# Hybrid attention block on one core: the high parts' cast moved directly behind the exponential, the gates' products behind the low parts

## The chip, the cores and the metric

One core of a Trainium2 chip runs the whole kernel. The metric is the device time of one execution in microseconds (us). The kernel before took 439.7 us as the median of 3 runs (439.3 to 441.55 us).

## The reference, cut to what matters

One encoder layer over 1024 tokens of width 1024. A single projection gives the columns of two head groups. Group A is two-dimensional neighbourhood attention (8 heads, a window of 8 x 16 on a grid of 16 rows and 64 columns, with a learned relative bias). Group B is windowed grouped-query attention (8 query heads, 2 key/value heads, |i - j| <= 128, rotary positions, a sink logit in the softmax). Each group's output is multiplied by SiLU of its gate columns, the two are concatenated and projected, and a LayerNorm follows.

```
h = einsum('bsd,de->bse', x, w_in)
q_a, k_a, v_a, z_a, q_b, k_b, v_b, z_b = split(h)
y_a = neighborhood_attention(q_a, k_a, v_a, rel_pos_bias)
y_b = windowed_gqa_with_sink(rotary(q_b), rotary(k_b), v_b, sink)
mixed = concatenate([y_a * silu(z_a), y_b * silu(z_b)])
x = layer_norm(alpha * x + einsum('bse,ed->bsd', mixed, w_out), ln_gain, ln_bias)
```

## The kernel before, in words

Float32 values are carried as a sum of two float16 parts, a high part (the rounded value) and a low part (the value less its high part), so that TensorE multiplies float16 tiles in three products. The program has three stretches: a first one of about 122 us that projects the values, scales the weights and projects the first six column blocks; the attention loop, from about 122 to 364 us; and the output projection with its LayerNorm. The change lies in the loop.

The loop at the end of `hybrid_block` (lines 1445 to 1536) runs over 128 blocks of scores, here numbered 0 to 127: group B first (blocks 0 to 63, four pairs of heads p of 16 blocks), then group A (64 to 127). In each step i the code issues, in this order:

- `stage_qk` for block i: TensorE forms the scores in a bank of `ps_s` (lines 889 and 890; there are four such banks), and VectorE masks them and takes the row's minimum `nm` (line 905, into `sn`);
- every fourth step `stage_ot` and `stage_pv`: m is the place in a group of four steps. At m = 0 TensorE transposes a finished group of outputs (line 1006, every second time) and multiplies the transposed probabilities `tr` of four blocks by the values (line 968), in banks of `ps_t`, of which there are two. `stage_pv` of group q comes at step 4q + 9, so the last of its four blocks has six steps to arrive. At m = 1 `stage_on` divides by the row sums (lines 977 and 984);
- `stage_z`: for group B the gates' product, four VectorE instructions per transposed bank (line 993). Two stand directly behind the transposes at m = 0; one at the head of each of the steps m = 2 and m = 3 (line 1454), ahead of that step's scores;
- up to two VectorE instructions from a queue, above all the low parts of the projected queries and keys (line 310, two per half of a column block, written `ks` or `qs`);
- `stage_tr` for block i - 1: ScalarE casts the probabilities to their high part (line 939, `split`), VectorE makes the low part from both (line 940), and a transposing DMA on SyncE's queue writes `tr` (line 942). `split` has six buffers, `tr` nine;
- ScalarE work with priority 0 from a queue, among it the first cast of a pair of queries or keys (line 304);
- `stage_exp` for block i: ScalarE's exponential, back into the block's bank of `ps_s` (line 921), in group B with the row sum read from the accumulator;
- more ScalarE work from the queue: the second cast of the pair of queries or keys (line 304; VectorE's line 310 waits for both), casts of weights (line 241, for which GpSimd then makes the low parts, lines 246 and 247), of rotated queries (line 306, GpSimd's line 312 behind them), of gated outputs (line 1171) and others;
- GpSimd's work, and between these the matmuls of the projections (line 443), dealt out evenly over the steps.

Each engine executes its own instructions in the order in which they are issued, so a step's order in the code is the order in each engine's queue. A block's way is thus: scores, `sn` with `nm`, exponential, high part, low part, transposing DMA, values.

Of the kernel before, what the change touches and what calls it, by code (L numbers as in the profile page):

```python
# [12 lines left out]
AF = mybir.ActivationFunctionType  # L13
ALU = mybir.AluOpType
# [10 lines left out]
PSCALE = 2.0 ** 14  # L25
# [40 lines left out]
def hybrid_block(ctx, tc, xT, x, wt, wv, wo, bias, sink, gain, lbias, cos, sin, bmask, out):  # L66
    nc = tc.nc
# [118 lines left out]
    def book(eng, work):  # L186
        if clock["step"] is not None:
            due[eng] = max(due[eng], at_step(clock["step"]))
        due[eng] += work
# [4 lines left out]
    def pop(eng, n, top=1, same=False):  # L194
        q = queues[eng]
        ready = [op for op in q if op.prio <= top and all(
            d.step is not None and d.step + d.lag < clock["step"] + (same and op.prio == 0 and d.eng == "act")
            and (eng != "sp" or d.fin + 1.0 < at_step(clock["step"]))
            and (eng != "act" or d.eng != "pool" or d.fin < at_step(clock["step"])) for d in op.deps)]
        for op in sorted(ready, key=lambda op: op.prio)[:n]:  # L200
            q.remove(op)
            op.emit()
# [622 lines left out]
    units = unit_list()  # L825
# [6 lines left out]
    st = {}  # L832
# [78 lines left out]
    def stage_exp(u):  # L911
        c = used(u)
        c = slice(c[0], c[1] + (u[0] == "b"))
        book("act", 0.2 + 0.0008 * (c.stop - c.start) + (0.2 if u[0] == "b" else 0))
        sn, nm = st.pop((u, "sn")), st.pop((u, "nm"))
        pt = st.pop((u, "ps"))
        k = units.index(u) % 4
        if k == 0 and u[0] == "b":
            st[units.index(u) // 4, "sm"] = ap.tile([128, 4], F32, tag="sm", name="sm", bufs=4)
        acc = st[units.index(u) // 4, "sm"][:, k:k + 1] if u[0] == "b" else None  # L920
        nc.scalar.activation(pt[:, c], sn[:, c], AF.Exp, bias=nm, scale=-1.0, accum_out=acc)  # L921
        st[u, "p"] = pt

    def stage_tr(u):
        n, m = geom(u)
        pt = st.pop((u, "p"))
        hl = split[units.index(u) % NSPLIT]
        c = slice(*used(u))
        book("act", 0.06 + 0.00086 * (c.stop - c.start))
        book("dve", 0.07 + 0.00108 * (c.stop - c.start))  # L930
        s = 384 - 128 * m
        if u[0] == "b":
            b = b_span(u)[0]
            if b == 7:
                nc.vector.memset(hl[:, 384:448], 0.0)
            if b == 4 and u[1] > 0:
                nc.vector.memset(hl[:, 320:384], 0.0)
        h, l = (hl[:, o + c.start:o + c.stop] for o in (s, 384))
        nc.scalar.activation(h, pt[:, c], AF.Copy, scale=PSCALE)  # L939
        nc.vector.scalar_tensor_tensor(l, pt[:, c], PSCALE, h, op0=ALU.mult, op1=ALU.subtract)  # L940
        tr = ap.tile([128, 6, 128], F16, tag="tr", name="tr", bufs=BH)
        nc.sync.dma_start(tr[:, :2 * m, :], hl[:, s:s + 256 * m], transpose=True)
        st[u, "tr"] = tr
# [42 lines left out]
    def stage_z(n):  # L986
        for _ in range(n if st.get("z") else 0):
            ps, k, h, e, m = st["z"].pop(0)
            o = ps.rearrange("p (b h c) -> p b h c", h=2, c=64)
            r = slice(64 * e, 64 * e + 64)  # L990
            z = zt[k][r, 512 * h:512 * h + 512].rearrange("p (b m c) -> p b m c", m=2, c=64)[:, :, m]
            book("dve", 0.42)
            nc.vector.scalar_tensor_tensor(z, o[64 * m:64 * m + 64, :, e], z_col(k)[r], z, op0=ALU.mult, op1=ALU.mult)

    def stage_ot(q):
        g, p, j, h = quad(q)
        if g == "b":
            j, h = h, j
        if j == 0:
            return  # L1000
        need(*stk_ops.get(f"zb{p}" if g == "b" else f"z{p}", ()))
        ps = bank("t")
        book("dve", 0.67 if g == "a" else 0)
        o = on.pop((g, p, h))
        for i in range(4):
            nc.tensor.transpose(ps[:, 128 * i:128 * i + 128], o[:, 2 * i:2 * i + 2].rearrange("p h e -> p (h e)"), identf)  # L1006
        if g == "b":
            st["z"] = [(ps, 4 + p, h, e, m) for e in range(2) for m in range(2)]
            stage_z(2)
        else:  # L1010
            z = zt[p].rearrange("p (r c) -> p r c", c=GW)[:, :, 32 * h:32 * h + 32]
            nc.vector.scalar_tensor_tensor(z, ps.rearrange("p (c r) -> p r c", r=ROWS), z_col(p), z,
                                           op0=ALU.mult, op1=ALU.mult)
# [204 lines left out]
    LT, LP = LTT, LPP  # L1218
# [226 lines left out]
    for i in range(-LD, NU + LO):  # L1445
        if 0 <= i + LD < NU:
            stage_load(units[i + LD], i)
        if i < 0:
            continue
        clock["step"] = i  # L1450
        per, h = divmod(i, 16)
        bulk["step"] = i
        if (i - LP - 3) % 4 > 1:
            stage_z(1)
        if i == VA_AT:
            gather_v(0)
        if i in SCAN_LD:
            n, b = divmod(NSCAN + SCAN_LD.index(i), 4)
            wo_load(SCAN[n], b, *scans[-4:-3])
            wo_scan(SCAN[n], b)  # L1460
        if i >= T_GO and i % 4 == 0 and len(scans) == 16 and all(op.step is not None and op.fin + 3 < at_step(i) for op in scans):
            wo_scale()
            scans.clear()
            t_prep(0)
            for b in range(4):
                wo_load(1, b, t_low[(0, 1, 3, 2)[b]])
            t_prep(1)
        if i in B_LD:
            n = B_LD.index(i)
            b_load(n, w_ops[NL - 5 + n] if n < 5 else b_ops[n - 5])  # L1470
        if i in B_AT:
            b_split(B_AT.index(i))
        if i in M_AT:
            m_queue(M_AT.index(i))
        if i == M2_AT:
            m_kq(2, ("A11", "A12", "A21", "A22"))
        if i == M3_AT:
            m_kq(3, ("A11", "A21"))
        if i == 129:
            t_soon(0)  # L1480
            x_soon(0)
            t_soon(3)
            x_soon(4)
            x_soon(1)
            t_soon(1)
            t_soon(2)
        if bulk["last"] == i:
            sp_at.append(i)
        if i >= 118:
            pop("sp", 3)  # L1490
        elif sum(j > i - 3 for j in sp_at) < 2:
            kept = len(queues["sp"])
            pop("sp", 1)
            if len(queues["sp"]) < kept:
                sp_at.append(i)
        if i < NU:
            u = units[i]
            if u[0] == "b" and u[3] == 0:
                need(*[o for j in range(2) for o in stk_ops[f"b{u[1]}", j, u[2]]])
            if u[0] == "a" and u[3] == 0:  # L1500
                need(*stk_ops[u[1], u[2], 0], *stk_ops[u[1], u[2], 1])
            stage_qk(u)
        q, m = divmod(i - LP - 3, 4)
        if i >= Q30 + 2:
            q, m = (NU // 4 - 2, i - Q30 - 2) if i < Q30 + 4 else divmod(i - LP - 3, 4)
        elif i >= Q30:
            q, m = -1, 0
        if m == 0 and 0 <= q - 1 < NU // 4:
            stage_ot(q - 1)
        if m == 0 and 0 <= q < NU // 4:  # L1510
            stage_pv(q)
        kept = len(queues["dve"])
        pop("dve", 2, 0)
        if m > 1 and len(queues["dve"]) == kept and i not in DVE_ADD and i < DVE_ADD[-1] and due["dve"] + DVE_OWN < at_step(i + 1):
            fill_in("dve")
        if 0 <= i - LT < NU:
            stage_tr(units[i - LT])
        pop("act", 1, 0)
        pump_to(i + F1)
        if 0 <= q < NU // 4:  # L1520
            g, p, j, h = quad(q)
            if g == "a" and p < 3 and (j, h, m) == VA_STEP:
                gather_v(p + 1)
        if m == 1 and 0 <= q < NU // 4:
            stage_on(q)
        pop("dve", ND, same=True)
        if i < NU:
            stage_exp(units[i])
        held = [op.prio for op in queues["act"] if op.prio <= 1]
        pop("act", NA if 0 in held or i < 105 and len(held) < 5 else 2)  # L1530
        pop("pool", NP)
        for eng in ("pool", "act", "dve")[:3 if i in DVE_ADD or len(scans) and i <= T_GO + 8 else 2]:
            for _ in range(2):
                if free_at(eng, ROOM[eng]):
                    fill_in(eng)
        pump_to(i + 1)
# [78 lines left out]
```

## Time and profile before

| | |
|---|---|
| median of 3 runs | 439.7 us (439.3 to 441.55) |
| the profiled execution, its whole time | 440.44 us |
| its span, first to last instruction | 438.6 us |
| VectorE instructions for the gates' product (line 993) | 32, 15.4 us in all |
| casts of queries and keys on ScalarE (line 304) | 32, 576 to 592 ns each |
| low parts of queries and keys on VectorE (line 310) | 32, 677 to 695 ns each |
| transposing DMA, issue to landing | 2.3 to 6.5 us, median 3.7 |

The profile is of one execution. An engine's busy time is the time in which it had an instruction under way; PE is TensorE's matmuls, PEld its weight loads, which run beside them, DVE is VectorE, ACT ScalarE, POOL GpSimd and SPq SyncE's DMA queue. In a row of the waits stand the time waited in all, the number of waits and the longest. In a row of the timeline stand the start in us, the duration in us, engine, line and tiles, how many instructions are merged into the row, and in brackets the engine's idle time ahead of it with what ended it.

### The profile page before, as it was taken

The numbers are of one execution on the slowest core, as the hardware profiler recorded it, in microseconds if no ns is written. First come the engines' busy times: TensorE is split into PE (matmuls) and PEld (weight loads), VectorE is DVE, ScalarE is ACT, GpSimd is POOL, SyncE is SP. The second block draws the span as 40 slices with busy tenths as digits, with TensorE's granted clock in tenths as the row PEclk, the third lists the DMA queues.
The fourth block names the chain that finished last, engine by engine and source line by source line (L and its number), as shares of the span: only waits on it lengthen the run. The fifth ranks groups of instructions, "written<-read, shape, count | busy, mean of one in ns | idle before, by whom it ended". The sixth has DMA issues, their size and how long they took to land.

```text
span 438.6 us, 9414 instructions
## 1 busy us (share of the span) xinstructions
PE 431.6 (98%) x3225; PEld 252.7 (58%) x3225; DVE 335.3 (76%) x852; ACT 309.9 (71%) x665; POOL 280.8 (64%) x300
## 2 busy tenths in 40 slices
PE   9999999999999999999999998999999999999996
PEld 8997754444445655565656564655656555444445
DVE  5977976775967888988888897978787755675455
ACT  5849789668678988787978769888889773332321
POOL 0100074668438658779988899797989881058585
PEclk9999999999999999999999999999999999999999
DMA  8922469995329999875899999989899969811113
GB/s 272 404 84 61 137 231 334 242 292 177 124 47 196 205 187 206 190 160 123 138 169 235 188 188 218 212 184 191 142 198 220 169 121 339 332 48 73 72 73 121
DMA packets 128817, 80.10 MB, mean 183 GB/s; under 512 B 97280, under 2 KB 106496, under 8 KB 128768
## 3 DMA queue, kind: packets, MB, share of 16 engines
q1 hardware_dynamic: 128624, 79.30, 75.3%
q8 instruction: 25, 0.41, 0.4%
q14 instruction: 24, 0.20, 0.1%
q10 hardware_dynamic: 144, 0.20, 0.1%
HBM read 47.97 MB, written 8.42 MB: 129 GB/s over the span
## 4 chain that ended last, share of the span: by engine, by line
PE 78%; POOL 5%; DMA 5%; ACT 4%; DVE 4%; issue 3%; SPq 0%; POOLq 0%; ACTq 0%
PE ps_pj L443 36%; PE ps_s L1240 8%; PE ps_s L550 6%; PE ps_t L968 6%; PE ps_pj L1240 4%; PE ps_s L889 3%; PE ps_s L890 3%; PE ps_pj L550 3%; PE ps_t L550 3%; PE ps_t L1240 2%; DMA vd<-vt 2%; DMA ws<-in_wt 2%; POOL xr L1349 2%; POOL xr L1350 2%; PE ps_t L1006 1%
## 5 line engine op out<-in xcount | busy, mean ns | idle before, releaser
L443 PE MATMUL ps_pj<-xf,wh 128*128 128x512 f16 x672 | 201.4, 379 | 0.0
L443 PE MATMUL ps_pj<-xf,wl 128*128 128x512 f16 x336 | 127.3, 379 | 0.0
L443 PEld LDWEIGHTS <-wh 128*128 128x128 f16 x672 | 63.6, 98 | 59.0 <-issue 1.1
L921 ACT ACTIVATE ps_s<-sn,nm 128x321 f32<-128x321 f32 (+3 forms) x128 | 68.4, 535 | 35.0 <-DVE nm L905 34.4
L940 DVE SCALAR_TENSOR_TENSOR split<-ps_s,split 128x320 f16<-128x320 f32 (+2 forms) x128 | 63.6, 497 | 19.5 <-ACT split L939 17.8
L246 POOL TENSOR_SCALAR wr<-wr,wsc 128x512 f32<-128x512 f32 x32 | 22.9, 715 | 67.8 <-ACT wh L241 63.7
L939 ACT ACTIVATE split<-ps_s 128x320 f16<-128x320 f32 (+2 forms) x128 | 55.5, 434 | 1.5
L443 PEld LDWEIGHTS <-wl 128*128 128x128 f16 x336 | 32.8, 98 | 37.9
L905 DVE CUSTOM_DVE_ANT_0 sn<-ps_s,bias,sg 128x368 f32<-128x368 f32 (+1 forms) x64 | 36.3, 566 | 11.4 <-PE ps_s L890 11.2
L247 POOL TENSOR_TENSOR wl<-wr,wh 128x512 f16<-128x512 f32 x32 | 39.9, 1247 | 2.7
L905 DVE CUSTOM_DVE_ANT_0 sn<-ps_s,bm,nsk 128x320 f32<-128x320 f32 (+2 forms) x64 | 36.6, 572 | 3.0 <-PE ps_s L890 2.4
L968 PEld LDWEIGHTS <-tr 128*128 128x128 f16 (+1 forms) x1056 | 36.3, 98 | 4.1 <-DMA tr<-split 1.3
L889 PE MATMUL ps_s<-ks,qs 128*128 128x320 f16 (+3 forms) x128 | 38.2, 298 | 0.0
L890 PE MATMUL ps_s<-ks,qs 128*128 128x320 f16 (+3 forms) x128 | 38.2, 298 | 0.0
L1240 PEld LDWEIGHTS <-m 128*128 128x128 f16 x198 | 19.0, 98 | 20.9 <-issue 0.2
L360 POOL COPY ks<-ks 64x512 f16<-64x512 f16 x40 | 26.2, 656 | 3.0 <-DVE ks L312 0.6
L1275 DVE SCALAR_TENSOR_TENSOR xr<-ps_s,yc,xr 128x512 f32<-128x512 f32 (+1 forms) x22 | 15.8, 724 | 14.0 <-PE ps_s L1240 13.5
L1347 ACT ACTIVATE xr<-xr,nmr,rstd 128x1024 f32<-128x1024 f32 x6 | 7.4, 1240 | 27.0 <-POOL nmr L1294 27.0
L1240 PEld LDWEIGHTS <-A 128*128 128x128 f16 x162 | 15.2, 98 | 15.7
L550 PEld LDWEIGHTS <-xf 128*128 128x128 f16 x192 | 18.6, 98 | 7.3
L241 ACT ACTIVATE wh<-wr,wsc 128x512 f16<-128x512 f32 x32 | 22.7, 709 | 0.0
L1349 POOL TENSOR_TENSOR xr<-xr,gb 128x512 f32<-128x512 f32 x13 | 16.9, 1303 | 8.1 <-ACT xr L1347 8.1
(221 smaller groups left out, 910.2 us busy)
## 6 DMA issues: line engine op xcount, KB each, us to landing
wr<-in_wt SPq DMA_DIRECT2D x32, 256.0 KB, 3.2
ws<-in_wt SPq DMA_DIRECT2D x15, 512.0 KB, 6.9
wor<-in_wo SPq DMA_DIRECT2D x20, 256.0 KB, 3.9
xr<-in_x SPq DMA_DIRECT2D x8, 512.0 KB, 10.5
wob<-in_wo SPq DMA_DIRECT2D x14, 256.0 KB, 3.9
out<-xr SPq DMA_DIRECT2D x14, 256.0 KB, 2.0
bias<-in_bias SPq DMA_DIRECT2D x8, 440.0 KB, 4.2
wvraw<-in_wv SPq DMA_DIRECT2D x9, 320.0 KB, 5.6
```

Of the source, the lines that this page charges most:

```text
L247: nc.gpsimd.tensor_sub(l, raw, h)
L360: nc.gpsimd.tensor_copy(place(t, o, half, col), place(t, a, half, col))
L443: nc.tensor.matmul(ps, a[:, k % 4, :], mv, start=(k == 0 and i == 0), stop=(k == KT - 1 and i == 2))
L550: nc.tensor.matmul(ps[:, :320], lh[:, ts], rh[:, cs], start=(k == ko[0] and i == 0), stop=(k == ko[-1] and i == 2))
L889: nc.tensor.matmul(ps[:, :n], q, sl[0], start=True, stop=False)
L890: nc.tensor.matmul(ps[:, :n], q, sl[1], start=False, stop=True)
L905: nc.vector.tensor_tensor_reduce(sn[:, at0:at0 + n], ps[:, :n], bias_t, sg[:, c:c + 1], init, op0=ALU.add, op1=ALU.min, accum_out=nm)
L921: nc.scalar.activation(pt[:, c], sn[:, c], AF.Exp, bias=nm, scale=-1.0, accum_out=acc)
L939: nc.scalar.activation(h, pt[:, c], AF.Copy, scale=PSCALE)
L940: nc.vector.scalar_tensor_tensor(l, pt[:, c], PSCALE, h, op0=ALU.mult, op1=ALU.subtract)
L968: nc.tensor.matmul(ps[:, w * m:w * m + e], a, b_, start=(i == 0), stop=(i == len(mms) - 1))
L1240: nc.tensor.matmul(ps[:, cs], lh[:, 128 * t:128 * t + 128], rh[:, cs], start=(fresh and e == 0 and n == 0), stop=(e == len(terms) - 1 and ...
```

## The change

`stage_tr` is cut in two. The cast to the high part becomes `stage_hi` and is issued for block i directly behind block i's exponential, ahead of the casts that ScalarE takes from its queue in that step; before, it was issued in step i + 1 behind them. The low part and the DMA stay where they were. The gates' products are taken out of `stage_ot` and from the head of the steps and are issued behind `stage_tr`: two at m = 0 and the third at m = 2; the fourth stays at the head of the step m = 3, and in VectorE's queue it now follows the third directly.

```
-    def stage_tr(u):
+    def stage_hi(u):
         n, m = geom(u)
         pt = st.pop((u, "p"))
         hl = split[units.index(u) % NSPLIT]
         c = slice(*used(u))
-        book("act", 0.06 + 0.00086 * (c.stop - c.start))
-        book("dve", 0.07 + 0.00108 * (c.stop - c.start))
         s = 384 - 128 * m
+        h, l = (hl[:, o + c.start:o + c.stop] for o in (s, 384))
+        nc.scalar.activation(h, pt[:, c], AF.Copy, scale=PSCALE)
+        st[u, "hl"] = hl, s, pt[:, c], h, l
+
+    def stage_tr(u):
+        n, m = geom(u)
+        hl, s, pt, h, l = st.pop((u, "hl"))
+        book("act", 0.06 + 0.00086 * pt.shape[1])
+        book("dve", 0.07 + 0.00108 * pt.shape[1])
...
-        h, l = (hl[:, o + c.start:o + c.stop] for o in (s, 384))
-        nc.scalar.activation(h, pt[:, c], AF.Copy, scale=PSCALE)
-        nc.vector.scalar_tensor_tensor(l, pt[:, c], PSCALE, h, op0=ALU.mult, op1=ALU.subtract)
+        nc.vector.scalar_tensor_tensor(l, pt, PSCALE, h, op0=ALU.mult, op1=ALU.subtract)
...
             st["z"] = [(ps, 4 + p, h, e, m) for e in range(2) for m in range(2)]
-            stage_z(2)
...
-        if (i - LP - 3) % 4 > 1:
+        if (i - LP - 3) % 4 == 3:
             stage_z(1)
...
             stage_tr(units[i - LT])
+        if m in (0, 2):
+            stage_z(2 - m // 2)
...
             stage_exp(units[i])
+            stage_hi(units[i])
```

In the built program the calls come out so that TensorE's, GpSimd's and SyncE's queues hold the same instructions in the same order as before. On ScalarE only the casts to the high part change their place, on VectorE only the gates' products; no instruction is added or removed.

On ScalarE, around the exponentials of blocks 70 and 71 (line 921; `split` is the high part, line 939 before and 931 now; `qs` is the cast of a half of a query block, `sn` the masked scores). Before:

```order
L304 ACTIVATE qs<-ps_pj 64x64x8
L921 ACTIVATE ps_s<-sn_1138,nm 128x384
L304 ACTIVATE qs<-ps_pj 64x64x8
L939 ACTIVATE split_1136<-ps_s 128x384
L921 ACTIVATE ps_s<-sn_1139,nm 128x256
L939 ACTIVATE split_1137<-ps_s 128x256
```

and now:

```order
L304 ACTIVATE qs<-ps_pj 64x64x8
L921 ACTIVATE ps_s<-sn_1138,nm 128x384
L931 ACTIVATE split_1136<-ps_s 128x384
L304 ACTIVATE qs<-ps_pj 64x64x8
L921 ACTIVATE ps_s<-sn_1139,nm 128x256
L931 ACTIVATE split_1137<-ps_s 128x256
```

The high part of block 70 now stands ahead of the second cast of the queries, not behind it. VectorE's queue is the same at this place: the two low parts of the queries (line 310) stand there ahead of block 70's low part, before and now.

On VectorE, around the scores of block 43 (`split` the low part, line 940 before and 945 now; `z` the gates' product, line 993 before and 998 now; line 798 begins a row of scales that is issued once). Before:

```order
L378 STREAM_SHUFFLE rp_sw<-rp_raw 128x512
L993 SCALAR_TENSOR_TENSOR z_1287<-ps_t,zc,z_1287 64x4x64
L905 ISA sn_1139,nm<-ps_s,bm,nsk,sg 128x320
L905 ISA nm 128x1
L940 SCALAR_TENSOR_TENSOR split_1132<-ps_s,split_1132 128x320
L993 SCALAR_TENSOR_TENSOR z_1287<-ps_t,zc,z_1287 64x4x64
L798 TENSOR_REDUCE wog<-ps_t 128x1
```

and now:

```order
L378 STREAM_SHUFFLE rp_sw<-rp_raw 128x512
L905 ISA sn_1139,nm<-ps_s,bm,nsk,sg 128x320
L905 ISA nm 128x1
L945 SCALAR_TENSOR_TENSOR split_1132<-ps_s,split_1132 128x320
L998 SCALAR_TENSOR_TENSOR z_1287<-ps_t,zc,z_1287 64x4x64 x2
L798 TENSOR_REDUCE wog<-ps_t 128x1
```

The third of the four products has moved behind the block's low part; the fourth stands behind the same instructions as before.

## The prediction

> **What bounds the kernel now.** I read the busy times of the page first, then TensorE's waits, then the groups of the two engines that the change touches.
>
> ```profile
> span 438.6 us, 9414 instructions
> ...
> PE 431.6 (98%) x3225; PEld 252.7 (58%) x3225; DVE 335.3 (76%) x852; ACT 309.9 (71%) x665; POOL 280.8 (64%) x300
> ```
>
> TensorE is busy for 431.6 of 438.6 us. No instruction of it is added or taken away, so the change can only work through its waits. Those that fall into the attention loop are two:
>
> ```profile
> PE ps_t L968 <- DMA tr<-split: 1.2, 1, 1.2
> PE ps_t L968 <- DVE z L993: 0.7, 1, 0.7
> ```
>
> Once it waits 1.2 us for a transposed block of probabilities, once 0.7 us for a gates' product. **1.9 us is therefore the most that the loop can give**, 0.4% of the time; there is no such bound on what it can lose. A measurement of this kernel can tell about 0.5%, 2.2 us, from no change: below 437.5 us is faster, above 441.9 us slower.
>
> ```profile
> L921 ACT ACTIVATE ps_s<-sn,nm 128x321 f32<-128x321 f32 (+3 forms) x128 | 68.4, 535 | 35.0 <-DVE nm L905 34.4
> L940 DVE SCALAR_TENSOR_TENSOR split<-ps_s,split 128x320 f16<-128x320 f32 (+2 forms) x128 | 63.6, 497 | 19.5 <-ACT split L939 17.8
> ```
>
> Off TensorE, VectorE's low parts wait 17.8 us in all for ScalarE's high parts, and the exponentials wait 34.4 us for VectorE's minima: the two engines hold each other up. The change goes at the 17.8 us.
>
> **The change part by part.** *The gates' products* (32, nothing added): where the fourth stands, the same instructions stand ahead of it as before, so in VectorE's sum the move is nothing. It could gain or lose one product's time (0.49 us, a row below) where a block's scores or low part is awaited; both ends stay in the range, the value is 0.
>
> *The high part behind the exponential* takes away waits of the low part, and makes every cast that stood between the two later by one high part. What that is worth is read at the two places where TensorE waits.
>
> *Place A, 201 us, the gates' product.*
>
> ```profile
> 190.00 0.49 DVE L940 SCALAR_TENSOR_TENSOR split<-ps_s,split 128x320 f16<-128x320 f32 x1 [0.69 <-ACT split L939]
> ...
> 191.63 0.49 DVE L940 SCALAR_TENSOR_TENSOR split<-ps_s,split 128x320 f16<-128x320 f32 x1 [0.62 <-ACT split L939]
> ...
> 195.00 0.49 DVE L940 SCALAR_TENSOR_TENSOR split<-ps_s,split 128x320 f16<-128x320 f32 x1 [0.22 <-ACT split L939]
> ...
> 198.49 0.49 DVE L940 SCALAR_TENSOR_TENSOR split<-ps_s,split 128x320 f16<-128x320 f32 x1 [0.53 <-ACT split L939]
> ...
> 201.76 0.49 DVE L993 SCALAR_TENSOR_TENSOR z<-ps_t,zc,z 64x256 f32<-64x256 f32 x1
> ...
> 202.31 1.21 PE L968 MATMUL ps_t<-vb,tr 128*128 128x64 f16 x36 [0.70 <-DVE z L993]
> ```
>
> Between 190.0 and 198.5 us four low parts wait, 0.69 + 0.62 + 0.22 + 0.53 = 2.06 us. Were these waits simply gone, the product would end over 0.70 us sooner and TensorE's wait with it: gain 0.70. Against it stands a second chain, through GpSimd:
>
> ```profile
> 186.63 0.53 ACT L921 ACTIVATE ps_s<-sn,nm 128x321 f32<-128x321 f32 x1 [1.90 <-DVE nm L905]
> ...
> 187.19 0.71 ACT L241 ACTIVATE wh<-wr,wsc 128x512 f16<-128x512 f32 x1
> 187.81 0.41 ACT L939 ACTIVATE split<-ps_s 128x320 f16<-128x320 f32 x1
> ...
> 188.06 0.69 POOL L246 TENSOR_SCALAR wr<-wr,wsc 128x512 f32<-128x512 f32 x1 [0.89 <-PE ps_t L968]
> ...
> 190.62 1.16 POOL L312 TENSOR_TENSOR qs<-rp_raw,qs 64x512 f16<-64x512 f32 x1
> ...
> 191.83 0.10 PEld L889 LDWEIGHTS <-qs 128*128 128x128 f16 x1 [0.25 <-POOL qs L312]
> ```
>
> GpSimd stands idle until the weights' cast of 187.19 us is done, works without a stop from then to the query tile `qs`, and TensorE takes that tile 0.05 us after it is made. With the high part ahead, the cast ends 0.41 us later, and so does `qs`: a new wait of about 0.4 us, unless the exponential at 186.63 comes earlier. It waits for VectorE, whose last low parts of keys ahead of it (line 310) themselves wait for casts that are now later. Place A lies between -0.7 and +0.4; I take the middle, **-0.2 us**.
>
> *Place B, 268 us, the transposed block.*
>
> ```profile
> 233.12 0.53 ACT L921 ACTIVATE ps_s<-sn,nm 128x321 f32<-128x321 f32 x1
> ...
> 237.10 0.59 ACT L304 ACTIVATE ks<-ps_pj 64x512 f16<-64x512 f32 x1
> ```
>
> ```profile
> 234.75 0.49 DVE L940 SCALAR_TENSOR_TENSOR split<-ps_s,split 128x320 f16<-128x320 f32 x1 [0.56 <-ACT split L939]
> ...
> 236.13 0.49 DVE L940 SCALAR_TENSOR_TENSOR split<-ps_s,split 128x320 f16<-128x320 f32 x1 [0.43 <-ACT split L939]
> ...
> 237.72 1.41 DVE L310 SCALAR_TENSOR_TENSOR ks<-ps_pj,ks 64x512 f16<-64x512 f32 x2
> ```
>
> ```profile
> 248.01 0.58 ACT L921 ACTIVATE ps_s<-sn,nm 128x384 f32<-128x384 f32 x1 [1.48 <-DVE nm L905]
> 248.53 0.70 ACT L241 ACTIVATE wh<-wr,wsc 128x512 f16<-128x512 f32 x1
> 249.14 0.47 ACT L939 ACTIVATE split<-ps_s 128x384 f16<-128x384 f32 x1
> ...
> 251.98 0.59 ACT L304 ACTIVATE qs<-ps_pj 64x512 f16<-64x512 f32 x1
> 252.60 0.49 ACT L939 ACTIVATE split<-ps_s 128x384 f16<-128x384 f32 x1
> 252.99 0.47 ACT L921 ACTIVATE ps_s<-sn,nm 128x256 f32<-128x256 f32 x1
> 253.49 0.38 ACT L939 ACTIVATE split<-ps_s 128x256 f16<-128x256 f32 x1
> ```
>
> ```profile
> 249.64 0.56 DVE L940 SCALAR_TENSOR_TENSOR split<-ps_s,split 128x384 f16<-128x384 f32 x1 [0.68 <-ACT split L939]
> ...
> 251.04 0.56 DVE L940 SCALAR_TENSOR_TENSOR split<-ps_s,split 128x384 f16<-128x384 f32 x1 [0.33 <-ACT split L939]
> ...
> 252.61 1.39 DVE L310 SCALAR_TENSOR_TENSOR qs<-ps_pj,qs 64x512 f16<-64x512 f32 x2
> ```
>
> In both stretches ScalarE works without a stop, and VectorE's pair of low parts of keys or queries (line 310) begins as the second cast of line 304 ends: 237.10 + 0.59 = 237.69 against 237.72, and 251.98 + 0.59 = 252.57 against 252.61. The waits of 0.56, 0.43, 0.68 and 0.33 us ahead of them are not late work but room: VectorE has to wait for that cast anyhow. And the change puts a high part ahead of it.
>
> What ScalarE's stretch gains in length: first the high part that moves ahead of the second cast, 0.38 us at 237.7 and 0.49 at 252.6. Second, the joins. A cast that does not read what stands ahead of it begins before that one's end: 248.53 + 0.70 = 249.23, and the high part begins at 249.14, 0.09 sooner. Directly behind its exponential it begins 0.03 later than that one's end: 252.99 + 0.47 = 253.46 against 253.49. So each block whose high part had a cast ahead of it loses about 0.12 us of ScalarE. There are two such blocks in either stretch besides the one of the second cast.
>
> ScalarE: Activation LUTs, a page of the Trainium skill, says in its section What ACT_TABLE_LOAD costs that back-to-back ACTIVATEs overlap by about 93 ns; it makes no exception for one that reads the other's result. The trace agrees at 249.14 and differs at 253.49; by the page the joins would cost nothing, and the total below would be 0.5 us less.
>
> The sum for B: the first stretch is longer by 0.38 + 2 x 0.12 = 0.62, so line 310 begins 0.6 us later. From 237.72 to 249.64 VectorE is without a wait of note, so this stays, and the exponential at 248.01, which waits for VectorE, is 0.6 late. The second stretch adds 0.49 + 2 x 0.12 = 0.73. Together 1.35; I take 1.2, as the scores of a step m = 2 now stand ahead of the third gates' product and start their exponential a little sooner.
>
> ```profile
> 254.65 1.21 SPq L942 DMA_TRANSPOSE tr<-split  x1
> ...
> 264.58 2.56 SPq L942 DMA_TRANSPOSE tr<-split  x2
> ```
>
> ```profile
> 269.88 0.45 PE L968 MATMUL ps_t<-va,tr 128*128 128x65 f16 x9 [1.16 <-DMA tr<-split]
> ```
>
> Line 310 of 252.6 us stands ahead of block 70's low part, and that ahead of the DMA at 254.65; from there to the DMA at 264.58 SyncE's queue is never idle for more than 0.4 us, and that DMA is the one that TensorE waits for at 269.88. So TensorE's 1.16 us become 2.4. Bounds: if ScalarE makes up for it and all four waits are regained, the wait goes whole, -1.16; if nothing is made up, +1.35. I take **+1.2 us**, by the row that decides, the second cast of 251.98.
>
> ```profile
> L993 DVE SCALAR_TENSOR_TENSOR z<-ps_t,zc,z x32: 470/484/493, 150.7 to 261.9; 64x256 f32<-64x256 f32 x32
> ```
>
> Behind 262 us no product of group B's gates is left, VectorE has room again, and what TensorE has lost stays lost. Sum: -0.2 + 1.2 = **+1.0 us**. The profiled execution took 440.44 us, 1.84 us of it outside the span, and would take 441.4. It lies 0.74 us above the median of the runs; from that, 439.7, the forecast is **440.7 us**.
>
> **The rivals.** *The waits go and nothing takes their place.* Then both of TensorE's waits go: -0.70 - 1.16 = -1.9, 437.8 us. For it speaks that four waits before place A come to 2.06 us and only 0.70 are needed; against it, that VectorE's pairs start at the very end of the second cast.
>
> *Slower: each pair of queries or keys costs TensorE.*
>
> ```profile
> 250.83 0.27 PE L889 MATMUL ps_s<-ks,qs 128*128 128x256 f16 x1
> ```
>
> The scores at 250.83 need the bank that block 68's low part (249.64 + 0.56 = 250.20) gives back: 0.63 us of room. That is the point: once VectorE is later than that, it is TensorE that waits at each further pair, for the scores and not only for `tr`. Of the 16 pairs of line 310 about eight, those between 220 and 290 us, lie where VectorE has no time to spare; at 0.43 us each, a high part, that is +3.4 us, 443.1. For it speaks that my 1.2 us are more than the room; against it, that VectorE waits, for all that, 17.8 us before the change.
>
> *It does nothing*: the blocks wait elsewhere, and the time is 439.7.
>
> **How the numbers follow.** The forecast (440.7, its own range 439.9 to 441.8) has a chance of 0.50, the first rival 0.22, the second 0.16, no effect 0.12. Faster by over 0.5% takes the end of the first rival in which more than the two waits goes: 0.06. Slower by over 0.5% is the second rival and the upper edge of the forecast, 0.16 + 0.04 = 0.20. The rest, 0.74, lies within 0.5%. The range reaches from the first rival's 437.8, less 0.2 for the runs' own spread, to the second rival's 443.1.
>
> **What would show it.**
>
> ```profile
> DVE ks L310 <- ACT ks L304: 0.7, 1, 0.7
> ```
>
> Right: the waits of the low parts for the high parts (17.8 us) nearly gone; in their place waits of line 310 for line 304, of which there is one before, of 0.7 us; TensorE's wait for `tr` near 268 us about 2.4 us, or waits for the scores' bank there; the product's wait near 201 us smaller. Wrong: no wait of line 310, and TensorE without a stop from 190 to 270 us (the first rival); or TensorE's waits spread over every pair between 220 and 300 us (the second). A wait at a place of which I do not speak, in the output projection above all, would be wrong too.

## The result, and the profile after

The changed kernel takes **442.85 us** (median of 6 runs, 442.14 to 443.8) against 440.14 us before (6 runs): a ratio of 1.0052, 95% interval 1.0031 to 1.0073, so 2.3 us slower, between 1.4 and 3.2. (The two medians differ by 2.7 us; the text goes by the ratio, here and below.) The forecast was 440.7 us, that is 1.0 us slower; the time lies outside the forecast's own range and nearest to the second rival, 443.1 us. The whole range holds it only because it reaches as far as that rival, which had a chance of 0.16.

Three rows of the page of the changed kernel: the span, the engines, and the low parts, whose line 940 is line 945 now.

```profile
span 440.8 us, 9414 instructions
...
PE 432.5 (98%) x3225; PEld 251.9 (57%) x3225; DVE 334.5 (76%) x852; ACT 316.1 (72%) x665; POOL 280.5 (64%) x300
...
L945 DVE SCALAR_TENSOR_TENSOR split<-ps_s,split 128x320 f16<-128x320 f32 (+2 forms) x128 | 63.5, 496 | 14.8 <-ACT split L931 13.2
```

The span is 2.2 us longer than before. The low parts still wait 13.2 us for the high parts, where 17.8 us were to be nearly gone.

TensorE's waits in the changed kernel (line waited at, what ended it, us in total, times, longest):

```profile
PE ps_t L973 <- DMA tr<-split: 1.1, 1, 1.1
...
PE ps_s L889 <- DVE split L945: 0.8, 2, 0.6
...
PE ps_t L973 <- DVE z L998: 0.3, 1, 0.3
PE ps_s L889 <- DVE sn L902: 0.3, 1, 0.3
```

The wait for the gates' product has shrunk from 0.7 to 0.3 us and the one for the transposed block is what it was, 1.1 us after 1.2. New are the rows at line 889: the scores wait for VectorE's low parts, each of which gives back the bank that the scores four blocks later take. The row that names `sn` is of this kind too: those scores, of block 66, start 0.06 us behind the end of block 62's low part (240.39 + 0.42 = 240.81).

```profile
240.39 0.42 DVE L945 SCALAR_TENSOR_TENSOR split<-ps_s,split 128x256 f16<-128x256 f32 x1
...
240.87 0.33 PE L889 MATMUL ps_s<-ks,qs 128*128 128x368 f16 x1 [0.27 <-DVE sn L902]
```

VectorE's own waits show why the low parts are late:

```profile
DVE split L945 <- ACT split L931: 13.2, 29, 1.3
...
DVE ks L310 <- ACT ks L304: 6.5, 8, 1.2
...
DVE qs L310 <- ACT qs L304: 4.9, 7, 1.4
```

The pairs of low parts of keys and queries wait 6.5 + 4.9 = 11.4 us for ScalarE's second cast, where before there was one wait of 0.7 us. Three engines' rows at one such pair, from the timeline of the changed kernel (start, duration, idle time ahead in brackets):

```profile
253.23 0.57 ACT L921 ACTIVATE ps_s<-sn,nm 128x384 f32<-128x384 f32 x1
253.83 0.49 ACT L931 ACTIVATE split<-ps_s 128x384 f16<-128x384 f32 x1
254.35 0.59 ACT L304 ACTIVATE qs<-ps_pj 64x512 f16<-64x512 f32 x1
...
254.97 1.39 DVE L310 SCALAR_TENSOR_TENSOR qs<-ps_pj,qs 64x512 f16<-64x512 f32 x2 [1.11 <-ACT qs L304]
256.40 0.56 DVE L945 SCALAR_TENSOR_TENSOR split<-ps_s,split 128x384 f16<-128x384 f32 x1
...
257.01 0.32 PE L889 MATMUL ps_s<-ks,qs 128*128 128x368 f16 x1 [0.65 <-DVE split L945]
```

ScalarE has block 70's high part ready at 253.83 + 0.49 = 254.32 and the second cast at 254.94. VectorE asks for them the other way round: first the pair, which needs the second cast, then the low part, which needs the high part. It stands idle for 1.11 us although the low part could have been made from 254.32 on; the low part ends at 256.96 and TensorE's scores, which need the bank that it gives back, start at 257.01 after 0.65 us of waiting.

To see where the time went, take the same matmuls in both traces: the first scores of the loop, those of blocks 65 and 86, and those of block 90, well behind the last such wait. Before, and in the changed kernel:

```profile
122.33 0.25 PE L889 MATMUL ps_s<-ks,qs 128*128 128x192 f16 x1
...
237.31 0.32 PE L889 MATMUL ps_s<-ks,qs 128*128 128x368 f16 x1
...
279.36 0.32 PE L889 MATMUL ps_s<-ks,qs 128*128 128x368 f16 x1
...
287.07 0.32 PE L889 MATMUL ps_s<-ks,qs 128*128 128x368 f16 x1
```

```profile
122.49 0.25 PE L889 MATMUL ps_s<-ks,qs 128*128 128x192 f16 x1
...
237.34 0.32 PE L889 MATMUL ps_s<-ks,qs 128*128 128x368 f16 x1
...
281.43 0.32 PE L889 MATMUL ps_s<-ks,qs 128*128 128x368 f16 x1
...
289.13 0.32 PE L889 MATMUL ps_s<-ks,qs 128*128 128x368 f16 x1
```

Between the first and the last TensorE needs 164.74 us before and 166.64 us now, 1.90 us more, and next to nothing is lost behind. Nearly all of it arises between blocks 65 and 86: 42.05 us before, 44.09 now. These are single profiles. A second one of the kernel before (at the end of this text) needs 1.04 us more than the first for the whole stretch, but only 0.30 more, 42.35 us, between blocks 65 and 86, so the loss there stands out from both. The rows of the waits above show only 0.6 us of it (1.1 + 0.8 + 0.3 + 0.3 after 1.2 + 0.7): a row counts from the end of the matmul ahead, which the profile models, and short waits are not listed.

### The profile page after: what moved, and what is told of

Read it like the earlier page. It is cut to its first block, busy times and chain, and to the rows that moved or that the text cites. A ratio compares the mean times of both kernels' runs of the same rounds, so it can differ in the third digit from the quotient of the medians.

```text
span 440.8 us, 9414 instructions
## 1 busy us (share of the span) xinstructions
PE 432.5 (98%) x3225; PEld 251.9 (57%) x3225; DVE 334.5 (76%) x852; ACT 316.1 (72%) x665; POOL 280.5 (64%) x300
## 4 chain that ended last, share of the span: by engine, by line
PE 68%; ACT 11%; DVE 8%; issue 5%; POOL 5%; DMA 2%; SPq 1%; POOLq 0%; DVEq 0%; ACTq 0%
PE ps_pj L443 32%; PE ps_s L1244 8%; PE ps_s L550 6%; PE ps_t L973 4%; PE ps_pj L1244 4%; ACT ps_s L921 3%; PE ps_pj L550 3%; PE ps_t L550 3%; PE ps_t L1244 2%; PE ps_s L889 2%; PE ps_s L890 2%; ACT split L931 2%; DVE sn L905 2%; POOL xr L1353 2%; POOL xr L1354 2%
## 5 line engine op out<-in xcount | busy, mean ns | idle before, releaser
L945 DVE SCALAR_TENSOR_TENSOR split<-ps_s,split 128x320 f16<-128x320 f32 (+2 forms) x128 | 63.5, 496 | 14.8 <-ACT split L931 13.2
L931 ACT ACTIVATE split<-ps_s 128x320 f16<-128x320 f32 (+2 forms) x128 | 56.9, 444 | 4.1
```

Of the source, the lines that this page charges most:

```text
L945: nc.vector.scalar_tensor_tensor(l, pt, PSCALE, h, op0=ALU.mult, op1=ALU.subtract)
```

## The experiments

The first theory was the second rival's: **the second cast** comes a high part later, VectorE's pair with it, then the low part behind the pair, the bank, and the scores. Against it stood the **joins** (0.12 us of ScalarE lost wherever a high part reads the exponential just made, the other half of the forecast's sum) and the **gates' products** in their new place. Each kernel was timed in alternation with the kernel before; a ratio is against that, with its 95% interval.

**Only the 16 exchanges.** In 16 steps the change puts the high part ahead of a second cast of keys or queries. Here that is all that is done; ScalarE's other high parts and the products stay as before. The edit against the changed kernel, with the products put back:

```
+    def ready0():
+        return any(op.prio == 0 and all(
+            d.step is not None and d.step + d.lag < clock["step"] and (d.eng != "pool" or d.fin < at_step(clock["step"]))
+            for d in op.deps) for op in queues["act"])
...
     def stage_tr(u):
+        if (u, "p") in st:
+            stage_hi(u)
...
             stage_exp(units[i])
-            stage_hi(units[i])
+            if ready0():
+                stage_hi(units[i])
```

> The kernel before with one part of the change: in the 16 steps in which ScalarE makes the second cast of a pair of queries or keys behind the exponential, the high part of the block is issued ahead of that cast; everywhere else, and for the gates' products, the order of before. Theory (the second cast comes a high part later, VectorE's pair of low parts with it, and the next scores wait for their bank): the whole loss comes back with these 16 exchanges, 442.1 to 443.1 us, with TensorE's waits for a low part or a minimum ahead of scores (line 889) of 0.8 us or more in all, between 235 and 290 us. Rival (the joins: 98 high parts each lose 0.12 us of ScalarE where they read the result just made): nothing here, 439.8 to 440.5.

442.3 us, ratio 1.0038 (1.0025 to 1.0050). Its waits:

```profile
PE ps_t L980 <- DMA tr<-split: 1.4, 1, 1.4
...
PE ps_s L889 <- POOL qs L312: 0.5, 1, 0.5
...
PE ps_s L889 <- DVE split L952: 0.2, 1, 0.2
...
DVE ks L310 <- ACT ks L304: 4.0, 7, 1.2
DVE qs L310 <- ACT qs L304: 3.1, 7, 0.6
```

Sixteen exchanges of two neighbours on one engine, of some 9,400 instructions, make the kernel 1.7 us slower: the joins are not needed for a loss. TensorE's waits ahead of scores for a low part come to 0.2 us in this profile and not to the 0.8 expected; the 7.1 us of line 310 are there. So this profile does not show where all of the 1.7 us fall.

**All but the 16 exchanges.** The changed kernel with the second cast ahead of the high part again:

```
             stage_exp(units[i])
-            stage_hi(units[i])
         held = [op.prio for op in queues["act"] if op.prio <= 1]
-        pop("act", NA if 0 in held or i < 105 and len(held) < 5 else 2)
+        kept = len(queues["act"])
+        pop("act", 1, 0)
+        kept -= len(queues["act"])
+        if i < NU:
+            stage_hi(units[i])
+        pop("act", (NA if 0 in held or i < 105 and len(held) < 5 else 2) - kept)
```

> The changed kernel with the second cast of queries or keys put back ahead of the high part in those 16 steps, all other high parts directly behind their exponentials and the gates' products as changed. Theory of the second cast: no loss, 439.5 to 440.7 us, and line 310 waits for line 304 under 2 us in all. Rival of the joins: the loss stays, 442 to 443 us.

439.11 us, ratio 0.9972 (0.9957 to 0.9986). Not only is the loss gone: the kernel is 1.2 us faster than before. All the joins outside the 16 steps are in it, so whatever they cost, the early high parts gain more. Line 310 still waits 3.0 + 0.6 us, more than the 2 expected.

**One part alone.** The edits: the products' three lines put back in the changed kernel; the same three lines changed in the kernel before.

> Only the high parts moved, the gates' products as before. Theory of the second cast: 442.2 to 443.2 us, as the changed kernel. Rival (the gates' products, now behind the low part, hold up TensorE's banks): half of the loss or more is gone, under 441.5 us.

443.38 us, ratio 1.0060 (1.0046 to 1.0074): the high parts alone carry the whole loss.

> Only the gates' products moved, the high parts as before. Theory of the second cast: 439.8 to 440.6 us, no change. Rival of the gates' products: 441.2 us or more.

440.68 us, ratio 1.0008 (0.9996 to 1.0021): no change that can be measured.

**VectorE's order altered instead.** If only the late pair's place ahead of the low part hurts, then the changed kernel should be cured by making the low part first, with ScalarE left as the change has it:

```
         kept = len(queues["dve"])
+        if 0 <= i - LT < NU:
+            stage_tr(units[i - LT])
         pop("dve", 2, 0)
...
         if 0 <= i - LT < NU:
-            stage_tr(units[i - LT])
+            book("act", 0.06 + 0.00086 * st["own"])
+            book("dve", 0.07 + 0.00108 * st["own"])
```

The two `book` lines leave `stage_tr`, which notes the width in `st["own"]`, so that the plan of the queues stays the same.

> The changed kernel with VectorE's order altered: the low part of the block and its transposing DMA stand ahead of what VectorE takes from its queue in that step (the pair of low parts of queries or keys, and four other instructions), not behind it; ScalarE's order is that of the change. Theory (what costs is not the late pair itself but the block's low part and bank that stand behind it on VectorE): the loss is gone, 439 to 440.5 us, and TensorE has no wait at line 889 between 235 and 290 us. Rival (ScalarE is what is short, and the second cast late delays the exponentials and minima whatever VectorE's order): 441.5 to 443 us. Second rival: the pair is late for the scores' next column block or for GpSimd's copies (line 360), a new wait there.

438.92 us, ratio 0.9975 (0.9960 to 0.9990). The second cast stands behind the high part as in the changed kernel, and nothing is lost. The same pair as above, in this kernel's timeline:

```profile
252.75 0.49 ACT L931 ACTIVATE split<-ps_s 128x384 f16<-128x384 f32 x1
253.26 0.59 ACT L304 ACTIVATE qs<-ps_pj 64x512 f16<-64x512 f32 x1
...
253.27 0.56 DVE L944 SCALAR_TENSOR_TENSOR split<-ps_s,split 128x384 f16<-128x384 f32 x1 [0.49 <-ACT split L931]
253.88 1.39 DVE L310 SCALAR_TENSOR_TENSOR qs<-ps_pj,qs 64x512 f16<-64x512 f32 x2
```

VectorE makes the low part while ScalarE makes the second cast, which ends at 253.85, and the pair starts at 253.88 without a wait. VectorE's idle time here is 0.49 us instead of 1.11, and TensorE has no wait for VectorE between 235 and 290 us.

**Both cures at once.** The second cast ahead of the high part, and the low part ahead of the pair.

> The second cast of queries and keys ahead of the high part on ScalarE and the low part ahead of the pair on VectorE. Theory: the pair no longer waits nor is waited for, 438.5 to 439.8 us, no better than the second cast alone (439.1 us) by more than 0.5 us, since TensorE's one long wait left, for the transposed block near 268 us, has been 1.1 to 1.6 us in every run. Rival (a low part that comes sooner starts its DMA sooner): that wait falls under 0.7 us and the time under 438.5 us.

441.72 us, ratio 1.0035 (1.0022 to 1.0049). Here the first theory falls: the second cast stands ahead of the high part again, as in the kernel before, the low part stands ahead of the pair, and the loss is back. The same pair again:

```profile
253.19 0.59 ACT L304 ACTIVATE qs<-ps_pj 64x512 f16<-64x512 f32 x1
253.80 0.49 ACT L931 ACTIVATE split<-ps_s 128x384 f16<-128x384 f32 x1
...
254.33 0.56 DVE L944 SCALAR_TENSOR_TENSOR split<-ps_s,split 128x384 f16<-128x384 f32 x1 [1.10 <-ACT split L931]
254.91 1.39 DVE L310 SCALAR_TENSOR_TENSOR qs<-ps_pj,qs 64x512 f16<-64x512 f32 x2
...
256.45 0.59 PE L443 MATMUL ps_pj<-xf,wh 128*128 128x512 f16 x2 [0.41 <-DVE qs L310]
```

It is the mirror image. VectorE now waits 1.10 us for the high part while the second cast lies ready from 253.78 on; low part and pair both come late, and TensorE waits for the bank of the projection that the pair gives back. The theory that was left is the **crossed order**: it costs to let ScalarE make two results in one order and VectorE take them in the other, whichever result comes first.

**The cross made and undone on the kernel before.** Two kernels test that without the other high parts: VectorE's exchange alone (the cross from the other side), and both exchanges (no cross, though the second cast is as late as in the first experiment).

> The kernel before with VectorE's order alone altered: in the 16 steps with a pair of queries or keys (and four others) the low part of the block stands ahead of the pair, while ScalarE still makes the second cast ahead of the high part. Theory (a loss comes wherever ScalarE makes two results in one order and VectorE takes them in the other, whichever engine is altered): 441.3 to 442.6 us, with waits of TensorE at the scores (line 889) or for the bank of the projection (line 443) between 235 and 290 us. Rival (only a late second cast costs): no loss, 439.3 to 440.5 us.

440.98 us, ratio 1.0021 (1.0007 to 1.0036): slower, though by less than the theory's range. The waits of TensorE that the theory named are not in the list of this profile either. What the list has is the wait of the low parts, 28.2 us where the kernel before has 17.8, and the timeline shows scores that start as soon as a late low part is done (250.12 + 0.56 = 250.68), 0.05 us behind it:

```profile
DVE split L939 <- ACT split L938: 28.2, 53, 1.2
...
250.12 0.56 DVE L939 SCALAR_TENSOR_TENSOR split<-ps_s,split 128x384 f16<-128x384 f32 x1 [0.68 <-ACT split L938]
...
250.73 0.27 PE L889 MATMUL ps_s<-ks,qs 128*128 128x256 f16 x1
```

> The kernel before with both exchanges in those 16 steps: the high part ahead of the second cast on ScalarE, the low part ahead of the pair on VectorE; all else as before. Theory of the crossed order: the two agree again, 439.2 to 440.6 us, although the second cast is as late as in the first experiment (442.3 us). Rival (what gains is that all the high parts are early, and that covers the exchange): 441 us or more.

439.64 us, ratio 0.9996 (0.9979 to 1.0013): the loss of the first experiment is gone by a second exchange.

**The products again, and the kernel before again.**

> The second cast of queries and keys ahead of the high part, all other high parts directly behind their exponentials, the gates' products where they were before the change. Theory (the place of the gates' products is worth nothing): 438.8 to 440 us, as with the products moved (439.1 us). Rival (their move gives 0.5 to 1 us as soon as the high parts are early): 439.6 us or more.

439.53 us, ratio 0.9987 (0.9973 to 1.0002).

> All high parts directly behind their exponentials, the low part ahead of the pair on VectorE, the gates' products where they were before the change. Theory (the place of the gates' products is worth under 0.6 us): 438.4 to 439.6 us. Rival (their new place behind the low part is what gains): 440 us or more.

439.5 us, ratio 0.9983 (0.9968 to 0.9999). Both lie in the theory's range, though close to the rival's: the new place of the products gives nothing that can be measured.

> The kernel before, unchanged, to see what two sets of executions of one kernel differ by and which of TensorE's waits recur. 439.5 to 440.7 us; the wait for the transposed block near 268 us (1.2 us) and that for the gates' product near 201 us (0.7 us) recur, that of 0.84 us at line 267 ahead of the loop need not.

439.85 us, ratio 0.9994 (0.9982 to 1.0006). Its long waits:

```profile
PE ps_t L968 <- DMA tr<-split: 0.9, 1, 0.9
PE ps_t L968 <- DVE z L993: 0.7, 1, 0.7
...
PE ps_s L889 <- POOL qs L312: 0.2, 1, 0.2
```

The two of the loop recur to within 0.3 us. A wait at line 267 does not; in the first profile's list it stands with 0.5 us.

All of it side by side; "cross" means that ScalarE's order of high part and second cast is not VectorE's of low part and pair:

| other high parts | ScalarE first | VectorE first | cross | ratio to before |
|---|---|---|---|---|
| late | second cast | pair | no | 1 (the kernel before; again: 0.9994) |
| late | high part | pair | yes | 1.0038 |
| late | second cast | low part | yes | 1.0021 |
| late | high part | low part | no | 0.9996 |
| early, products moved | high part | pair | yes | 1.0052 (the change) |
| early, products moved | second cast | low part | yes | 1.0035 |
| early, products moved | second cast | pair | no | 0.9972 |
| early, products moved | high part | low part | no | 0.9975 |

All four crossed kernels of the table are slower than before, each with an interval above 1; none of the uncrossed is. With the products in their old place the three kernels with early high parts give 1.0060 (cross), 0.9987 and 0.9983 (no cross).

How the cross reaches TensorE can be read in every profile in the same way, from the time between a low part's end and the start of the scores that take its bank, four blocks later. Between 220 and 290 us some scores start 0.05 to 0.06 us behind that end in each crossed kernel: six in the changed kernel, four in the first experiment, two with the high parts alone moved, two with both cures, three with VectorE's exchange alone. In the uncrossed kernels and with the products alone moved there are none; the shortest such time there is 0.14 us, and in the kernel before 0.63. With both cures TensorE waits for the bank of the projection as well, as shown above.

## Why the prediction came out as it did

- **What the kernel is bound by** held: TensorE's instructions and their order did not change, and the loss shows as matmuls that start late, though the rows of its waits hold only a part of it.
- **The mechanism** was named rightly: line 310 was to wait for line 304, and does, 11.4 us after 0.7. In the result this is the sum of two parts: the early high parts, with the products moved, are worth 1.2 us (0.9972), and the 16 crosses cost 3.5 us (1.0052 / 0.9972 = 1.0080). The forecast saw the cost only as a cast that is one high part late, and so did the second rival. The runs show that lateness by itself costs nothing (0.9975, 0.9996) as long as VectorE takes the results in the order in which they come.
- **Place A** was right in its steps. GpSimd's query tile came half a microsecond later, 191.12 after 190.62, and TensorE's weight load waited 0.59 us for it instead of 0.25; the product's wait halved:

```profile
192.33 0.10 PEld L889 LDWEIGHTS <-qs 128*128 128x128 f16 x1 [0.59 <-POOL qs L312]
...
191.12 1.15 POOL L312 TENSOR_TENSOR qs<-rp_raw,qs 64x512 f16<-64x512 f32 x1
...
202.30 1.21 PE L973 MATMUL ps_t<-vb,tr 128*128 128x64 f16 x36 [0.35 <-DVE z L998]
```

  The values at 202.30 started at 202.31 before; with the first scores 0.16 us later (122.49 after 122.33) that is a gain of 0.17 us, where -0.2 was forecast. To come so close was luck in part: the forecast took the middle of its bounds without a row that decides, and from the loop's first scores to this place the second profile of the kernel before needs 0.75 us more than the first (202.11 - 121.38 = 80.73 after 202.31 - 122.33 = 79.98).
- **Place B** is the step that failed. "So TensorE's 1.16 us become 2.4", it said; the wait for the transposed block stayed at 1.1. TensorE came to it later itself, held up at the scores before: the block's values start at 271.61 after 269.88, 1.73 us later, and nearly all of that was lost at the scores. The forecast had that point in hand (0.63 us of room for the scores' bank, and 1.2 us of lateness are more) but left it to the second rival because VectorE waited 17.8 us for high parts anyway. That argument was wrong: those waits did not give way, 13.2 us of them are left, and the room of 0.63 us for the bank shrank to 0.05 or 0.06 at six scores.
- **Why they are left** can be read at one block in the changed kernel's rows. Between a minimum and the high part lie the exponential and the cast, 0.57 + 0.49 us with the join at 251.24 and 251.84; VectorE has only the next block's scores to mask in that time, 0.59 us. How the whole 13.2 us divide was not measured; other casts have a part in them too.

```profile
251.24 0.57 ACT L921 ACTIVATE ps_s<-sn,nm 128x384 f32<-128x384 f32 x1
251.84 0.49 ACT L931 ACTIVATE split<-ps_s 128x384 f16<-128x384 f32 x1
...
251.24 0.59 DVE L905 CUSTOM_DVE_ANT_0 sn<-ps_s,bias,sg 128x368 f32<-128x368 f32 x1
...
252.37 0.56 DVE L945 SCALAR_TENSOR_TENSOR split<-ps_s,split 128x384 f16<-128x384 f32 x1 [0.53 <-ACT split L931]
```

- **The size of VectorE's lateness** was too small. The pair at 237.72 was to come 0.6 us later and that at 252.61 1.35; they came 1.23 and 2.36 later, at 238.95 and 254.97. The forecast let ScalarE's first stretch begin on time, though a pair ahead of it was already 0.67 us late, 227.89 before and 228.56 after, and 0.53 us of that were left at the stretch's first exponential, 233.12 before and 233.65 after:

```profile
228.56 1.39 DVE L310 SCALAR_TENSOR_TENSOR qs<-ps_pj,qs 64x512 f16<-64x512 f32 x2
...
238.95 1.41 DVE L310 SCALAR_TENSOR_TENSOR ks<-ps_pj,ks 64x512 f16<-64x512 f32 x2 [1.08 <-ACT ks L304]
```

- **The joins** have the 0.03 us that the prediction read from the kernel before: 251.24 + 0.57 = 251.81 against 251.84. The Trainium skill's page ScalarE: Activation LUTs gives an overlap of about 93 ns for back-to-back ACTIVATEs in its section What ACT_TABLE_LOAD costs. It does not appear at this place. The prediction's rule for the other casts, that one which does not read what stands ahead of it begins before that one's end, has exceptions: the second cast at 254.35 does not read the high part, and begins 0.03 us behind its end (253.83 + 0.49 = 254.32). In time the joins cost less than the early high parts gain, as the kernel with nearly all of both is the faster one; the two were not measured apart.
- **The second rival** priced the pairs at 3.4 us, eight of them at a high part each. By the experiments the crosses cost 3.5 us beside the early high parts, against which the 1.2 us gain stood that it left out. In place of eight steps of 0.43 us the two profiles show five: at the scores of block 65 TensorE is 0.03 us late, and at those that start at 240.41, 249.32, 255.41, 264.48 and 279.36 us before it is 0.46, 0.79, 1.60, 1.75 and 2.07 us late.
- **The gates' products** were put at 0, and no run tells their move from 0: 1.0008 alone, and 0.08% to 0.15% in its favour in three comparisons with early high parts, inside the intervals.

Why the crosses cost less with the other high parts late (0.9 and 1.7 us) than with them early (2.6 to 3.5 us) was not tested. The rows show that line 310 waits less there, 7.1 us in the first experiment after 11.4 in the changed kernel.

## What to carry to other kernels

Where one engine makes several results that another takes, keep the two orders the same. Before an instruction is moved ahead of its neighbours on one engine, look up in which order the other engine takes what both make; if it is the opposite one, exchange the takers too, or leave the makers. And a wait that the rows show is not room to be used up until it is clear which chain it belongs to: here 13.2 of 17.8 us stayed when the high parts were made as early as they can be.

## What the runs showed of the hardware

VectorE did not reach past an instruction that waited: its low part at 256.40 had all that it reads from 254.32 on and stood behind the pair for 2.08 us. The Trainium skill's page PSUM — Partial Sum Buffer calls the queues of ScalarE, VectorE and GpSimd strict FIFO, first in, first out (section Engine vs sequencer instructions). This case agrees for VectorE.

Not expected was how far two executions of the same instructions differ. The stretch from the loop's first scores to those of block 90 took 164.74 us in the first profile of the kernel before, and in the second 165.78 us, while the medians of their runs agree within 0.1%. The rows of the second:

```profile
121.38 0.25 PE L889 MATMUL ps_s<-ks,qs 128*128 128x192 f16 x1
...
237.11 0.32 PE L889 MATMUL ps_s<-ks,qs 128*128 128x368 f16 x1
...
279.46 0.32 PE L889 MATMUL ps_s<-ks,qs 128*128 128x368 f16 x1
...
287.16 0.32 PE L889 MATMUL ps_s<-ks,qs 128*128 128x368 f16 x1
```

A difference of 1 us in a stretch of this length, in one profile, is no evidence here, and the verdicts above rest on the times of the runs.
